# The residual of the first output projection: identity products in the sum's own bank, or transposes into a separate bank and an add on VectorE

## The chip, the core and the metric

The kernel runs on one core of a Trainium2 chip (trn2). The metric is the device time of one execution in microseconds (us). Before the change three runs took 3237.32, 3238.66 and 3239.86 us; their median is 3238.66 us.

## The reference

One step of a one-layer trunk over 640 frames: 512 of a prompt and 8 running streams of 16. With `h = rmsnorm(x)`, three mixers (GLA, gated delta net, RWKV-7) read columns of one projection `h @ w_in`, and then

```python
mix = jnp.matmul(jnp.concatenate([o_gla, o_gdn, o_rw], axis=-1), prm['w_out'][l])
x = x + mix
h = rmsnorm(x, prm['norm2_g'][l])
x = x + jnp.matmul(jax.nn.silu(jnp.matmul(h, w_ffn_gate)) * jnp.matmul(h, w_ffn_up), w_ffn_down)
y = rmsnorm(x, prm['final_norm_g'])
```

`x` is 640 x 2048 in float32, `w_out` 2048 x 2048. The change is in the line `x = x + mix`: how the old `x` gets into that sum.

## The kernel before

The kernel keeps activations transposed: 16 blocks of 128 columns, each a tile of 128 partitions x 640 frames. A float32 operand is split into a high part and the rest (`hi`, `lo`), and each product is three matmuls of 128x320: `hi` x high, `hi` x low, `lo` x high (lines 1388, 1389, 1390 in `dense`). They are called **dense products** below.

The stages follow each other: `norm1`, the mixers, the output projection in two halves (`outproj1` over 8 of the 16 blocks of the mixers' output, `outproj2` over the other 8), then the feed-forward part. The mixers' instructions all carry line 322, whatever they do; their order was worked out by a planner inside the program (class `Plan`). Everything behind them is put in order by the framework that builds the kernel: it takes an instruction when its inputs and its buffers are free, by priority, so `outproj1` starts while the last unit of the mixers (a gated delta head pair) still runs, and its dense products lie between that unit's small ones. Each engine then runs its list strictly in that fixed order, and waits where an instruction's inputs are late.

In PSUM the pool `pd` holds three tiles of 128x512 in float32, and the mixers' pool `mps` five (two `ma`, two `mm`, one `po`). `mps` is closed in `build` before `outproj1` is called; later pools get its places.

`outproj1` (line 1577) goes over 16 blocks m of output columns. For each it loads the 128 columns of `x` into a tile `xf` (frames on partitions, lines 1588 and 1590), loads two pieces of `w_out` and splits them (lines 1368, 1371 on ScalarE, 1372 on VectorE; three raw buffers and three `hi`/`lo` pairs in rotation), runs 48 dense products into two `pd` tiles (one for each half of the frames), and adds the residual: six products with the identity, `xf` as the left operand, which turn `xf` around and accumulate it into the same two `pd` tiles (line 1597; four of 128 columns, two of 64). Then ScalarE copies both halves over `xf` (line 1603). `mixparts` (lines 1570 to 1572) loads and splits the mixers' output. `outproj2` adds its own products to those tiles later with VectorE (line 1659).

Of the kernel before, what the change touches and what calls it, by code (L numbers as in the profile page):

```python
# [13 lines left out]
F32 = mybir.dt.float32  # L14
# [3 lines left out]
AF = mybir.ActivationFunctionType  # L18
ALU = mybir.AluOpType
AX = mybir.AxisListType  # L20
PSUM = bass.MemoryType.PSUM

T = 640
TP = 512
NT = 5
# [1313 lines left out]
class Trunk:  # L1339
# [70 lines left out]
    def build(self):  # L1410
        tc, nc, a, o = self.tc, self.nc, self.a, self.o
        ctx = ExitStack()
        with ctx:
            kp = ctx.enter_context(tc.tile_pool(name="kp", bufs=1))
            dp = ctx.enter_context(tc.tile_pool(name="dram", bufs=1, space=bass.MemoryType.DRAM))
            self.pd = ctx.enter_context(tc.tile_pool(name="pd", bufs=3, space=PSUM))
            ident = kp.tile([128, 128], F32, name="ident0")
            nc.sync.dma_start(out=ident, in_=self.cf_ap[:, CF_OFF["ident"][0]:CF_OFF["ident"][0] + 128])
            self.ident = ident
            mixd = dp.tile([16, 128, T], F32, name="mixd")  # L1420
            yd = dp.tile([16, 128, T], F32, name="yd")
            actd = dp.tile([22 * 7, 128, 320], F32, name="actd")
            mctx = ExitStack()
            bp = ctx.enter_context(tc.tile_pool(name="bp", bufs=1, side="right"))
            wctx = ExitStack()
            self.wp = wctx.enter_context(tc.tile_pool(name="wp", bufs=1, side="right"))
            self.free, self.where = [(bp, f"b{i}") for i in range(32)], {}
            h = [(self.take(), self.take()) for k in range(16)]
            self.cols = [kp.tile([128, sum(n for _, n in g)], F32, name=f"cols{i}") for i, g in enumerate(GROUPS)]
            self.norm1(h)  # L1430
            mc = mctx.enter_context(tc.tile_pool(name="mc", bufs=1))
            ms = mctx.enter_context(tc.tile_pool(name="ms", bufs=1))
            mps = mctx.enter_context(tc.tile_pool(name="mps", bufs=1, space=PSUM))
            self.mixers(h, mixd, (mc, ms, mps))
            self.give(*(t for x in h for t in x))
            mctx.close()
            bq = ctx.enter_context(tc.tile_pool(name="bq", bufs=1))
            places = [(bq, f"b{i}") for i in range(32, 57)]
            x2, xs = self.outproj1(mixd, KORDER, places)
            self.pe = ctx.enter_context(tc.tile_pool(name="pe", bufs=3, space=PSUM))  # L1440
            self.px = ctx.enter_context(tc.tile_pool(name="px", bufs=1, space=PSUM))
            self.fs = ctx.enter_context(tc.tile_pool(name="fs", bufs=1))
            with tc.tile_pool(name="fa", bufs=1) as self.fa:
                self.acts = Acts(self, actd)
                self.outproj2(KORDER[8:], xs, x2, self.col("norm2_g"), yd)
                self.gateup()
            wctx.close()
            self.down(yd)
# [125 lines left out]
            xs.append((hi, lo))  # L1574
        return xs

    def outproj1(self, mixd, ks, places):

        nc, a = self.nc, self.a
        ks, later = ks[:8], ks[8:]  # L1580
        xs = self.mixparts(mixd, ks)
        x2 = []
        for m in range(16):
            x = self.take()
            xf = x.bitcast(F32)
            with self.tc.high_priority(offset=WPRIO):
                c = slice(m * 128, (m + 1) * 128)
                nc.sync.dma_start(out=xf[:, 0:TP].rearrange("p (i c) -> p i c", i=4),
                                  in_=a["x_prompt"][0, :, c].rearrange("(i p) c -> p i c", p=128))
                nc.sync.dma_start(out=xf[:, TP:T], in_=a["x_sample"].rearrange("b t d -> (b t) d")[:, c])  # L1590

            def residual(ps):
                for i in range(NT):
                    for hf in range(2):
                        t0, t1 = max(128 * i, 320 * hf), min(128 * i + 128, 320 * hf + 320)
                        if t0 < t1:
                            nc.tensor.matmul(ps[hf][:, t0 - 320 * hf:t1 - 320 * hf], lhsT=xf[:, i * 128:(i + 1) * 128],
                                             rhs=self.ident[:, t0 - 128 * i:t1 - 128 * i], start=False,
                                             stop=t1 in (320, T))

            z = self.dense(self.wcols(a["w_out"][0], m * 128, ks), len(ks) // 4, self.halves(xs), extra=residual)
            for hf in range(2):
                nc.scalar.activation(xf[:, hf * 320:(hf + 1) * 320], z[hf], AF.Copy)
            x2.append(x)
            if m == 6:
                self.free += places
                xs2 = []
            if 6 <= m < 14:
                xs2 += self.mixparts(mixd, later[m - 6:m - 5])
        self.give(*(t for x in xs for t in x))  # L1610
        return x2, xs2
# [531 lines left out]
KORDER = [10, 11, 12, 13, 14, 15, 0, 1, 2, 3, 4, 5, 6, 7, 8, 9]  # L2143
# [31 lines left out]
```

## Time and profile before

| | |
|---|---|
| median of three runs | 3238.66 us |
| the profiled execution | 3239.36 us, span 3237.5 us |
| TensorE busy | 3162.8 us, 98% |
| TensorE weight loads | 3045.5 us, 94% |
| VectorE, ScalarE, GpSimd busy | 71%, 41%, 10% |
| granted TensorE clock, mean | 0.994 |
| HBM | 108 GB/s over the span |

A share of busy time is a mean over stages. A granted clock of 1.00 is the upper of TensorE's two levels (2.4 GHz), 0.50 the lower (1.2 GHz). Start times in a timeline are microseconds from the span's start; the time in brackets is idle time of that engine just before the row, with what ended it. A float32 product that isn't of the split kind is shown as two records, a transpose as one. The distance between the starts of two rows is what a product takes of the engine; the duration of a row includes the way through the array, and rows overlap.

### The profile page before, as it was taken

What the parts mean: (1) busy time and instruction counts of PE and PEld (TensorE: products, weight loads), DVE (VectorE), ACT (ScalarE), POOL (GpSimd) and SP (SyncE); (2) the same over time, 40 slices, a digit from 0 to 9 for tenths busy, and PEclk for the clock granted to TensorE, in tenths of its full rate; (3) what the DMA queues carried; (4) which work ended last, traced back from release to release, by engine and by line L of the source; (5) the groups of instructions that cost most, each with busy time, mean ns of one, the idle gap of its engine ahead of it and who ended that gap; (6) DMA issues with size and microseconds to landing.
All of it is one profiled execution on the core that took longest, in us unless ns stands there. A gap on an engine that the chain in (4) does not pass through costs nothing.

```text
span 3237.5 us, 61481 instructions
## 1 busy us (share of the span) xinstructions
PE 3162.8 (98%) x23589; PEld 3045.5 (94%) x23589; DVE 2307.0 (71%) x5672; ACT 1322.1 (41%) x2797; POOL 326.5 (10%) x521
## 2 busy tenths in 40 slices
PE   7999999999999999999999999999999999999997
PEld 6988888899999999999999999999999989999997
DVE  4677776664666677336888777777777788878786
ACT  4433333332333334335544344444443453434344
POOL 1111110000110000002000000000000032323221
PEclk9999999999999999999999999999999999999998
DMA  4222222222223235436433333333333376767675
GB/s 130 59 57 55 56 49 46 60 59 70 72 75 78 75 78 145 149 115 186 125 106 111 117 96 120 105 109 114 103 116 107 108 225 136 185 126 197 136 171 150
DMA packets 407528, 354.24 MB, mean 109 GB/s; under 512 B 26080, under 2 KB 390098, under 8 KB 406594
## 3 DMA queue, kind: packets, MB, share of 16 engines
q1 hardware_dynamic: 374098, 284.36, 30.3%
q0 software_dynamic: 32848, 65.96, 9.2%
q8 instruction: 184, 3.01, 0.4%
q14 instruction: 110, 0.90, 0.1%
q10 hardware_dynamic: 288, 0.01, 0.0%
HBM read 282.13 MB, written 68.11 MB: 108 GB/s over the span
## 4 chain that ended last, share of the span: by engine, by line
PE 84%; DVE 6%; issue 4%; DMA 3%; ACT 1%; POOL 1%; SPq 0%; DVEq 0%; POOLq 0%; ACTq 0%
PE d_r L322 22%; PE pw L1799 10%; PE pw L1800 10%; PE pw L1801 10%; PE mm_r L322 8%; PE dn L1962 4%; PE dn L1964 4%; PE dn L1963 4%; PE pd L1390 2%; PE pd L1388 2%; PE pd L1389 2%; PE ma_r L322 2%; PE po_r L322 1%; DMA dr<-in_w_ffn_down 1%; POOL yd L2066 1%
## 5 line engine op out<-in xcount | busy, mean ns | idle before, releaser
L322 PE MATMUL d_r<-b,hi_r 128*128 128x320 f32 (+1 forms) x3648 | 797.5, 317 | 0.7 <-ACT b L1529 0.7
L322 PEld LDWEIGHTS d_r<-b,hi_r 128*128 128x128 f32 (+1 forms) x3648 | 593.6, 188 | 22.4 <-issue 13.7
L322 PE MATMUL d_r<-b,lo_r 128*128 128x320 f32 (+1 forms) x1824 | 506.7, 317 | 0.0
L1799 PE MATMUL pw<-b,hi 128*128 128x320 f32 x1416 | 437.3, 309 | 0.0
L1800 PE MATMUL pw<-b,hi 128*128 128x320 f32 x1416 | 436.5, 308 | 0.2 <-DVE b L1635 0.2
L1801 PE MATMUL pw<-b,lo 128*128 128x320 f32 x1416 | 436.6, 308 | 0.0
L1963 PE MATMUL dn<-b,dh 128*128 128x320 f32 x1222 | 379.8, 311 | 7.3 <-DVE b L2104 7.3
L1964 PE MATMUL dn<-b,dl 128*128 128x320 f32 x1222 | 379.1, 310 | 7.2 <-DVE dl L1945 7.2
L1962 PE MATMUL dn<-b,dh 128*128 128x320 f32 x1222 | 378.7, 311 | 0.9 <-ACT dh L1944 0.9
L322 PEld LDWEIGHTS d_r<-b,lo_r 128*128 128x128 f32 (+1 forms) x1824 | 324.3, 188 | 7.5 <-issue 3.9
L1800 PE MATMUL pw<-b,hx 128*128 128x320 f32 x936 | 289.4, 309 | 0.0
L1799 PE MATMUL pw<-b,hx 128*128 128x320 f32 x936 | 289.2, 309 | 0.1
L1801 PE MATMUL pw<-b,lx 128*128 128x320 f32 x936 | 289.1, 309 | 0.0
L1800 PEld LDWEIGHTS pw<-b,hi 128*128 128x128 f32 x1416 | 265.5, 188 | 0.8 <-DVE b L1635 0.8
L1799 PEld LDWEIGHTS pw<-b,hi 128*128 128x128 f32 x1416 | 265.7, 188 | 0.2
L1801 PEld LDWEIGHTS pw<-b,lo 128*128 128x128 f32 x1416 | 265.7, 188 | 0.0
L322 DVE TENSOR_TENSOR lo_r<-raw_r,hi_r 128x512 fp32r<-128x512 f32 (+1 forms) x228 | 155.6, 683 | 145.3 <-ACT hi_r L322 104.8
L322 ACT ACTIVATE hi_r<-raw_r 128x512 fp32r<-128x512 f32 (+1 forms) x228 | 142.2, 624 | 256.4 <-PE d_r L322 236.3
L1963 PEld LDWEIGHTS dn<-b,dh 128*128 128x128 f32 x1222 | 230.3, 188 | 9.7 <-DVE b L2104 9.7
L1964 PEld LDWEIGHTS dn<-b,dl 128*128 128x128 f32 x1222 | 230.5, 189 | 8.4 <-DVE dl L1945 8.4
L1962 PEld LDWEIGHTS dn<-b,dh 128*128 128x128 f32 x1222 | 230.5, 189 | 1.4 <-ACT dh L1944 1.4
L1388 PE MATMUL pd<-b,hi 128*128 128x320 f32 x640 | 200.9, 314 | 3.4 <-ACT b L1571 1.9
(482 smaller groups left out, 6301.1 us busy)
## 6 DMA issues: line engine op xcount, KB each, us to landing
raw_r<-in_w_in SPq DMA_DIRECT2D x224, 256.0 KB
rw<-in_w_ffn_gate SPq DMA_DIRECT2D x84, 512.0 KB
rw<-in_w_ffn_up SPq DMA_DIRECT2D x84, 512.0 KB
b<-actd POOLq DMA_DIRECT2D x77, 320.0 KB, 7.0
dr<-in_w_ffn_down SPq DMA_DIRECT2D x32, 768.0 KB
actd<-s SPq DMA_DIRECT2D x132, 160.0 KB
raw<-in_w_out SPq DMA_DIRECT2D x80, 256.0 KB
yd<-t POOLq DMA_DIRECT2D x124, 160.0 KB, 4.8
```

What stands on the lines that cost most here:

```text
L322: self.made.append(op[2](*op[3], **op[4]))
L1388: nc.tensor.matmul(out, lhsT=hi[:, kk, :], rhs=xh, start=k == 0, stop=False)
L1389: nc.tensor.matmul(out, lhsT=hi[:, kk, :], rhs=xl, start=False, stop=False)
L1390: nc.tensor.matmul(out, lhsT=lo[:, kk, :], rhs=xh, start=False, stop=k == nk - 1 and not extra)
L1799: nc.tensor.matmul(ps, lhsT=hi[:, kk, :], rhs=bh, start=k == 0, stop=False)
L1800: nc.tensor.matmul(ps, lhsT=hi[:, kk, :], rhs=bl, start=False, stop=False)
L1801: nc.tensor.matmul(ps, lhsT=lo[:, kk, :], rhs=bh, start=False, stop=k == 7)
L1962: nc.tensor.matmul(ps, lhsT=hi[:, k], rhs=bh, start=k == 0, stop=False)
L1963: nc.tensor.matmul(ps, lhsT=hi[:, k], rhs=bl, start=False, stop=False)
L1964: nc.tensor.matmul(ps, lhsT=lo[:, k], rhs=bh, start=False, stop=k == c - 1)
L2066: nc.gpsimd.dma_start(out=yd[2 * p + i // 2][:, ones(i)], in_=z, accum_op=ALU.add)
```

## The change

The dense products of a block end the sum by themselves. The residual no longer goes through products with the identity: five transposes turn `xf` around into a PSUM tile of its own (`pt`, 640 columns of a 1024 column tile in a new pool `xt` with one buffer). ScalarE copies each half of `pt` over `xf`, and VectorE adds the `pd` tile to it.

```diff
-            x2, xs = self.outproj1(mixd, KORDER, places)
+            with tc.tile_pool(name="xt", bufs=1, space=PSUM, reuse_waits="tile") as xt:
+                x2, xs = self.outproj1(mixd, KORDER, places, xt)
...
-    def outproj1(self, mixd, ks, places):
+    def outproj1(self, mixd, ks, places, xt):
...
-            def residual(ps):
-                for i in range(NT):
-                    for hf in range(2):
-                        t0, t1 = max(128 * i, 320 * hf), min(128 * i + 128, 320 * hf + 320)
-                        if t0 < t1:
-                            nc.tensor.matmul(ps[hf][:, t0 - 320 * hf:t1 - 320 * hf], lhsT=xf[:, i * 128:(i + 1) * 128],
-                                             rhs=self.ident[:, t0 - 128 * i:t1 - 128 * i], start=False,
-                                             stop=t1 in (320, T))
-
-            z = self.dense(self.wcols(a["w_out"][0], m * 128, ks), len(ks) // 4, self.halves(xs), extra=residual)
+            z = self.dense(self.wcols(a["w_out"][0], m * 128, ks), len(ks) // 4, self.halves(xs))
+            pt = xt.tile([128, 1024], F32, name=self.name("xt"), tag="x")[:, 0:T]
+            for i in range(NT):
+                c = slice(i * 128, (i + 1) * 128)
+                nc.tensor.transpose(pt[:, c], xf[:, c], self.ident)
             for hf in range(2):
-                nc.scalar.activation(xf[:, hf * 320:(hf + 1) * 320], z[hf], AF.Copy)
+                c = slice(hf * 320, (hf + 1) * 320)
+                nc.scalar.activation(xf[:, c], pt[:, c], AF.Copy)
+                nc.vector.tensor_tensor(xf[:, c], xf[:, c], z[hf], ALU.add)
```

The lists of the engines move. In the changed file the lines behind `build` carry other numbers: 1597 is the transpose, 1600 ScalarE's copy, 1601 VectorE's add.

TensorE, where the last mixer unit's first correction products come (`mm_r` from `X_r` and `N_r`; `pd` are tiles of the dense products). Before:

```order
L1388 MATMUL pd_13436<-b_13251,hi_13440 128x320
L1389 MATMUL pd_13436<-b_13252,hi_13440 128x320
L322 MATMUL mm_r_400<-X_r_407,N_r_415 128x64 x4
L1390 MATMUL pd_13436<-b_13251,lo_13441 128x320
L1388 MATMUL pd_13437<-b_13233,hi_13440 128x320
L1389 MATMUL pd_13437<-b_13234,hi_13440 128x320
L1390 MATMUL pd_13437<-b_13233,lo_13441 128x320
L322 MATMUL mm_r_401<-Y_r_404,P_r_406 128x64 x4
L1388 MATMUL pd_13437<-b_13239,hi_13440 128x320
```

With the change:

```order
L1390 MATMUL pd_13365<-b_13272,lo_13403 128x320
L1388 MATMUL pd_13365<-b_13278,hi_13402 128x320
L1389 MATMUL pd_13365<-b_13279,hi_13402 128x320
L1390 MATMUL pd_13365<-b_13278,lo_13403 128x320
L322 MATMUL mm_r_400<-X_r_407,N_r_415 128x64 x4
L322 MATMUL mm_r_401<-Y_r_404,P_r_406 128x64 x4
L322 MATMUL mm_r_400<-X_r_407,N_r_415 64x32 x8
L322 MATMUL mm_r_401<-Y_r_404,P_r_406 32x32
L322 MATMUL mm_r_400<-P_r_406,Y_r_404 64x32 x8
```

Before, dense products of the blocks m = 2 and on stand between the mixers' products. With the change 72 dense products (48 of block 0 and the first half of the frames of block 1, tile `pd_13365`) stand ahead of this place, and none between the mixers' products from here on.

TensorE, at the mixers' last two products (`mm_r` from `SX_r` and `VS_r`). Before:

```order
L1388 MATMUL pd_13588<-b_13245,hi_13592 128x320
L322 MATMUL mm_r_400<-SX_r_410,VS_r_398 128x512
L1389 MATMUL pd_13588<-b_13246,hi_13592 128x320
L1390 MATMUL pd_13588<-b_13245,lo_13593 128x320
L1388 MATMUL pd_13588<-b_13251,hi_13592 128x320
L1389 MATMUL pd_13588<-b_13252,hi_13592 128x320
L1390 MATMUL pd_13588<-b_13251,lo_13593 128x320
L1388 MATMUL pd_13589<-b_13233,hi_13592 128x320
L322 MATMUL mm_r_401<-SX_r_410,VS_r_398 128x512
L1389 MATMUL pd_13589<-b_13234,hi_13592 128x320
```

With the change:

```order
L322 MATMUL mm_r_401<-ident_63,on_r_416 128x128
L322 MATMUL mm_r_400<-ident_63,on_r_416 128x128 x4
L322 MATMUL mm_r_400<-SX_r_410,VS_r_398 128x512
L322 MATMUL mm_r_401<-SX_r_410,VS_r_398 128x512
L1597 MATMUL xt_13352<-ident_63,b_13284 128x128 x5
L1597 MATMUL xt_13430<-ident_63,b_13362 128x128 x3
L1388 MATMUL pd_13366<-b_13236,hi_13369 128x320
L1389 MATMUL pd_13366<-b_13237,hi_13369 128x320
L1390 MATMUL pd_13366<-b_13236,lo_13370 128x320
```

Before, block 4 has begun by the mixers' last product (`pd_13588`, `pd_13589`), and four blocks have their residual. With the change the first transposes of all, those of block 0, stand behind the mixers' last product, and the second half of block 1 (`pd_13366`) behind them.

VectorE, later in `outproj1`, where the loop runs evenly (blocks 12 and 13), with the change:

```order
L1601 TENSOR_TENSOR b_14256<-b_14256,pd_14259 128x320
L1601 TENSOR_TENSOR b_14256<-b_14256,pd_14260 128x320
L1372 TENSOR_TENSOR lo_14465<-raw_14459,hi_14464 128x512
L1372 TENSOR_TENSOR lo_14510<-raw_14507,hi_14509 128x512
L1601 TENSOR_TENSOR b_14340<-b_14340,pd_14343 128x320
L1601 TENSOR_TENSOR b_14340<-b_14340,pd_14344 128x320
```

Before, VectorE's list has only the `lo` splits here; now two adds follow two splits in each block. From the first rows of `outproj2` to the end of the kernel, TensorE, VectorE and ScalarE have the same lists before and after, and GpSimd's is the same throughout; SyncE's differs in the places of some loads within `outproj1`.

## Rows read from the trace of the kernel before

**Rows 1.** Busy time of each engine, from the profile's page.

```profile
PE 3162.8 (98%) x23589; PEld 3045.5 (94%) x23589; DVE 2307.0 (71%) x5672; ACT 1322.1 (41%) x2797; POOL 326.5 (10%) x521
```

**Rows 2.** Busy time by engine, clock, DMA share in two windows of `outproj1`.

```profile
1288.50:1323.15 34.65, 34.46 (x281) 30.84 (x281) 15.16 (x38) 11.45 (x35) 1.12 (x2) 1.00 0.16 50
...
1324.40:1422.00 97.60, 97.60 (x702) 97.60 (x701) 21.20 (x30) 29.34 (x53) 1.04 (x3) 1.00 0.47 139
```

**Rows 3.** TensorE's timeline around a block's residual: start, duration, engine, line, operation.

```profile
1330.09 0.31 PE L1389 MATMUL pd<-b,hi 128*128 128x320 f32 x1
...
1336.83 0.31 PE L1390 MATMUL pd<-b,lo 128*128 128x320 f32 x1
1336.98 1.50 PE L1597 MATMUL pd<-ident,b 128*128 128x128 f32 x12
1338.23 0.39 PE L1388 MATMUL pd<-b,hi 128*128 128x320 f32 x1
1338.46 0.31 PE L1389 MATMUL pd<-b,hi 128*128 128x320 f32 x1
```

**Rows 4.** TensorE's timeline in norm1: five transposes between dense products.

```profile
30.14 0.31 PE L322 MATMUL d_r<-b,hi_r 128*128 128x320 f32 x1
30.29 0.71 PE L1522 MATMUL xpa<-ident,x 128*128 128x128 f32 x5
30.75 0.39 PE L322 MATMUL d_r<-b,hi_r 128*128 128x320 f32 x1
30.98 0.71 PE L1522 MATMUL xpa<-ident,x 128*128 128x128 f32 x5
```

**Rows 5.** Line 322 alone (the mixers): PE, PEld, DVE, ACT, POOL busy.

```profile
1281.30:1288.50 7.20, 0.00 (x1) 0.01 (x1) 5.05 (x43) 0.00 (x0) 0.53 (x1) 1.00 0.50 147
1288.50:1323.15 34.65, 19.29 (x158) 14.90 (x158) 11.92 (x33) 7.38 (x27) 1.12 (x2) 1.00 0.16 50
```

**Rows 6.** Lines 1388, 1389, 1390 alone: PE busy and count, PEld, until 1322.51.

```profile
1255.00:1322.51 67.51, 22.63 (x69) 12.91 (x69) 1.00 0.49 141
...
1255.00:1322.51 67.51, 22.05 (x68) 12.88 (x68) 1.00 0.49 141
...
1255.00:1322.51 67.51, 21.51 (x68) 12.83 (x68) 1.00 0.49 141
```

**Rows 7.** VectorE's and TensorE's timelines: the mixers' last chain, first and last steps.

```profile
1287.14 0.68 DVE L1372 TENSOR_TENSOR lo<-raw,hi 128x512 fp32r<-128x512 f32 x1
...
1288.50 1.10 PE L322 MATMUL mm_r<-X_r,N_r 128*128 128x64 f32 x8 [0.43 <-DVE X_r L322]
...
1319.14 0.60 PE L322 MATMUL mm_r<-ident,on_r 128*128 128x128 f32 x4
...
1320.60 1.12 PE L322 MATMUL mm_r<-SX_r,VS_r 128*128 128x512 f32 x2
...
1322.51 1.13 PE L322 MATMUL mm_r<-SX_r,VS_r 128*128 128x512 f32 x2
```

**Rows 8.** TensorE's timeline after an idle stretch, and a window of it.

```profile
1589.27 0.41 PE L1390 MATMUL pd<-b,lo 128*128 128x320 f32 x1 [2.47 <-DVE lo L1372]
...
1589.89 0.47 PE L1390 MATMUL pd<-b,lo 128*128 128x320 f32 x1
...
1593.26 0.30 PE L1388 MATMUL pd<-b,hi 128*128 128x320 f32 x1
...
1590.00:1592.00 2.00, 2.00 (x9) 2.00 (x8) 2.00 (x5) 0.00 (x0) 0.00 (x0) 0.50 0.51 146
```

**Rows 9.** ScalarE's copies and VectorE's split in a steady block; outproj2's add.

```profile
1338.01 0.94 ACT L1603 ACTIVATE b<-pd 128x320 f32<-128x320 f32 x2 [0.35 <-PE pd L1597]
...
1337.69 0.69 DVE L1372 TENSOR_TENSOR lo<-raw,hi 128x512 fp32r<-128x512 f32 x1 [2.83 <-ACT hi L1371]
...
L1603 ACT ACTIVATE b<-pd x32: 429/438/439, 1279.1 to 1422.3; 128x320 f32<-128x320 f32 x32
...
L1659 DVE TENSOR_TENSOR b<-b,pd x32: 469/487/490, 1425.8 to 1538.3; 128x320 f32<-128x320 f32 x32
```

## The prediction, made blind

> **What bounds the kernel now.** I read the page's busy times first: TensorE is busy for 98% of the span [rows 1], so what the change takes from TensorE or leaves it without work counts in full, unless something else ends a stage. Then the windows of this stage. From 1324.40 to 1422.00 us, most of `outproj1`, TensorE is busy for all 97.60 us, VectorE for 21.20, and the DMA engines for 0.47 of the time [rows 2]: TensorE alone is the bound there. Just before, while the last mixer unit finishes, TensorE is busy for 34.46 of 34.65 us as well [rows 2], but the reader should then look at the mixers' line alone: of these 34.65 us it fills 19.29, and from 1281.30 to 1288.50 it has no time on TensorE at all, while VectorE solves for `X_r` [rows 5]. What fills the rest is dense products and residuals of `outproj1`. They are a filler under a chain of small steps over TensorE, ScalarE and VectorE. Last I read the timelines, for what one piece takes and for what the chain waits on.
>
> **What the change removes.** Where the loop runs evenly a block's residual begins at 1336.98, where the next dense product would have stood (the one before began at 1336.83). The two dense products after it begin at 1338.23 and 1338.46 [rows 3]. So the way from 1336.98 to 1338.46 took 1.48 us with one dense product in it; dense products follow each other every 0.147 us (46 steps within a block, from 1330.09 to 1336.83 [rows 3]). The residual costs TensorE 1.33 us a block.
>
> **What it adds on TensorE.** Five float32 transposes of 128x128 stand between dense products in `norm1`: they begin at 30.29, the next dense product at 30.75 and what follows it at 30.98 [rows 4]. That is 0.69 us with one dense product in it, so 0.54 us a block. Each block thus saves 0.79 us, and 16 blocks 12.6 us, if nothing else moved. The Trainium skill, "TensorE: Matmul & The Clock Gate", section "Terms", says that transpose mode is four times as fast for float32. Both forms stream 640 columns, so by that rule a block's transposes would take 0.33 us and 16 blocks would save 16.0 us; the rows have a fixed part at each change of kind, and I stay with 0.54.
>
> **What it adds elsewhere.** ScalarE still copies two halves a block, 0.438 us each [rows 9]; only the source is another. VectorE gets 32 adds, of 0.487 us as in `outproj2` [rows 9], 15.6 us on an engine busy for 21.20 of 97.60 [rows 2]. They cost nothing as long as the `pd` tile is free in time. Block m+1 begins in the third tile, twelve dense products long, and then needs the tile of block m's first half. Counted from the end of block m's products, that need comes at 0.54 + 12 x 0.147 = 2.30 us. The tile is free after the transposes (0.46), the hand-over to ScalarE (0.35, the idle time in rows 9), the copy (0.44) and the add (0.49), 1.74 us, and about 1.9 with two short hand-overs. VectorE's list puts two splits ahead of the adds. The last of them began 0.71 us after the residual (1337.69 against 1336.98) and took 0.69 [rows 3, 9], so it ends at about 1.4 and the add at 1.9. The cover is 0.4 us; a further split in front would cost 0.3 us in that block.
>
> **What it moves, the large term.** The list of TensorE shows that all transposes stand behind the mixers' last product. Block 0 can't be finished without them, so its two `pd` tiles stay full, the first half of block 1 takes the third, and TensorE has run out of filler after 48 + 24 = 72 dense products. Before, by the mixers' last product at 1322.51 [rows 7], the three lines of the dense products had 69 + 68 + 68 = 205 records [rows 6], and four blocks had their residual. So 133 dense products, 133 x 0.147 = 19.5 us, lose their cover and come after the chain instead. Of the residuals, the four that lay under the chain gave nothing when removed; the other twelve give 12 x 1.33 = 16.0 us. All 16 sets of transposes come after it: 16 x 0.54 = 8.6 us. From this alone the end comes 19.5 - 16.0 + 8.6 = **12.1 us later**.
>
> **Three corrections.** First, the chain itself. Without dense products on TensorE and splits on VectorE in its way it gets shorter: the first `SX_r` products came at 1320.60, though what precedes them had run from 1319.14 for 0.60, so 0.86 us of filler lay between. A split of 0.68 ended just ahead of the `X_r` that TensorE waited for at 1288.50 [rows 7]. With a split earlier in the same stretch and smaller delays of the same kind I take 3 us. It can hardly be much more: the mixers' own times on TensorE, VectorE and ScalarE from 1288.50 to 1323.15 add up to 19.29 + 11.92 + 7.38 = 38.6 us in a window of 34.65 [rows 5], so little of it is waiting for others. Bounds: 0 and 8. Second, the restart. After the first transposes TensorE waits for a copy and an add (0.35 + 0.44 + 0.49 and two hand-overs, about 1.4 us) and has 0.3 us of block 1's transposes meanwhile: 1.1 us, once.
>
> Third, the clock. In this trace 2.47 us without work before 1589.27 were followed by 13 dense products in the 3.37 us from 1589.89 to 1593.26, 0.26 us each instead of 0.147, with a granted clock of 0.50, the 1.2 GHz level [rows 8]. That cost 3.37 - 1.91 = 1.5 us. With the change TensorE has nothing to do for the 7.2 us up to 1288.50, so the mixers' products that follow start at the lower level. Then they fill a little more than half of the time, and no row shows which level holds in such a stretch. Lower bound: one such drop, 1.5 us. Upper bound: all 19.29 us of the mixers on TensorE at half speed, 19.3 us more, the drop after it included. The row nearest to it is that of the single drop, which ended after 3.4 us of full work; here there is no full work until the end. Some of the products also lie beside the chain. I take a third, **6.5 us**. The Trainium skill, "TensorE: Matmul & The Clock Gate", section "HAM oscillation — how this bites in real kernels", describes that short bursts between waits start cold each time. By that rule the whole chain would run at the lower level, which is a rival below; rows 8 show the drop, and no run here shows such bursts.
>
> **The sum.** 12.1 - 3.0 + 1.1 + 6.5 = 16.7 us on the profiled execution's 3239.36: 3256.1. That execution is 0.7 above the median of the runs, 3238.66, so I predict 3255. What follows `outproj1` is in the same order as before, so I carry no later gain or loss.
>
> **The rivals.**
> - **One drop of the clock only.** TensorE returns to the upper level within the chain, as it did at 1593.26 [rows 8], and the term is 1.5: 12.1 - 3.0 + 1.1 + 1.5 = 11.7, so 3250. For it: the mixers take more than half of the time at full speed. Against: 7.2 us of nothing first, and every step waits for another engine. 0.21.
> - **The lower clock all along the chain.** About three quarters of the 19.29 us lie on the chain and double, 14 us, and the restart pays a drop of 1.5: 12.1 - 3.0 + 1.1 + 15.5 = 25.7, so 3264. The Trainium skill's rule, named above, would come out here. For it: no stretch of full work between 1288.50 and the transposes. 0.17.
> - **The bare chain contracts.** If the chain was slow because it queued behind filler, it ends much earlier alone. At the upper clock 12.1 + 1.1 = 13.2 us of contraction brings the time to 3239, and 20 us to 3232, faster than before. It decides from 13 us on. Against: its own work fills the window [rows 5], and TensorE waited for the chain, not the other way, where it began [rows 7]. 0.11 for anything near or beyond no change.
> - **The add holds the banks.** If VectorE is late by another split in each of 14 blocks, 14 x 0.3 = 4 us come on top, 3260. It is inside the range.
> - That the change doesn't do what it says I leave out: the lists have 16 sets of five transposes and 32 adds.
>
> **How the numbers follow.** The forecast, a clock that is low for part of the chain (3252 to 3261), has 0.51. The range 3245 to 3266 takes in the single drop, the forecast, and most of the low clock; it leaves out the contracting chain and the far end of the low clock, 0.17 together. This kernel's measurement tells about 0.2% (6.5 us) from no change: faster means under 3232, slower over 3245. Only a chain shorter by 20 us is faster, 0.03; the rest of that rival, and a single drop with a chain shorter than I take it, is the same, 0.09; all else is slower, 0.88.
>
> **What the profile after would show.** TensorE idle from about 1281 to 1288, with the wait put down to VectorE's `X_r`, and then line 322 alone until about 1320 to 1335, with gaps. The granted clock below 1.00 in that stretch is the third correction; its mean tells which of the three cases holds. The first transposes follow the `SX_r` products; from there a block takes 48 x 0.147 + 0.54 = 7.6 us in place of 8.4, with no waits of dense products on VectorE's adds. `outproj1` ends some 17 us later than before, and the rest keeps its length. I am wrong if dense products run between the mixers' products after 1290, if the clock stays at 1.00 through the idle stretch, if the blocks take over 7.7 us, or if the later stages change their length by over 2 us.

## The result, and the profile after

The changed kernel takes 3269.24 us (median of four runs, 3266.97 to 3270.61), the kernel before 3239.05 (four runs on the same chip, 3237.32 to 3239.86). The ratio is 1.0094, with a 95% interval from 1.0082 to 1.0106: slower by some 30 us. The forecast was 3255, its range ended at 3266. The sign is right; the size lies above the range.

The profiled execution took 3270.17 us with a span of 3268.2. The page's busy times answer to [rows 1]:

```profile
PE 3171.2 (97%) x23477; PEld 3048.8 (93%) x23477; DVE 2321.7 (71%) x5704; ACT 1320.3 (40%) x2797; POOL 326.2 (10%) x521
```

TensorE has 112 records fewer (12 per block for the residual before, 5 now) and is busy for 8.4 us *more*. Fewer records and more busy time point to work that ran slower; the rows below show where. TensorE's timeline from the hole to the restart answers to [rows 7] (start, duration, engine, line, operation; in brackets the idle time and what ended it):

```profile
1279.81 0.31 PE L1390 MATMUL pd<-b,lo 128*128 128x320 f32 x1
1288.00 1.97 PE L322 MATMUL mm_r<-X_r,N_r 128*128 128x64 f32 x8 [7.88 <-DVE X_r L322]
...
1327.37 1.44 PE L322 MATMUL mm_r<-ident,on_r 128*128 128x128 f32 x5 [3.88 <-ACT on_r L322]
1329.66 2.08 PE L322 MATMUL mm_r<-SX_r,VS_r 128*128 128x512 f32 x2 [0.84 <-DVE G_r L322]
1332.52 2.08 PE L322 MATMUL mm_r<-SX_r,VS_r 128*128 128x512 f32 x2 [0.79 <-DVE SX_r L322]
1334.39 1.27 PE L1597 MATMUL xt<-ident,b 128*128 128x128 f32 x5
1336.52 0.90 PE L1597 MATMUL xt<-ident,b 128*128 128x128 f32 x3 [0.85 <-ACT b L1600]
1337.07 0.62 PE L1388 MATMUL pd<-b,hi 128*128 128x320 f32 x1
```

TensorE runs out of dense products at 1280, waits 7.9 us for `X_r`, and has the mixers' chain alone until 1332.52, 10.0 us later than before (the chain begins 0.5 us sooner and is 10.5 us longer). Each of these mixers' rows takes almost twice as long as its counterpart in [rows 7]: 1.97 for 1.10, 2.08 for 1.13. The windows of TensorE give the reason (window, its length, busy time and records, granted clock, DMA share, GB/s):

```profile
1280.00:1284.00 4.00, 0.12 (x1) 0.83 0.97 278
1284.00:1288.00 4.00, 0.00 (x1) 0.50 0.01 2
1288.00:1292.00 4.00, 3.47 (x15) 0.50 0.00 0
...
1316.00:1320.00 4.00, 4.00 (x19) 0.50 0.00 0
...
1340.00:1344.00 4.00, 4.00 (x28) 0.91 0.50 138
1344.00:1348.00 4.00, 4.00 (x30) 1.00 0.82 240
```

From 1284 to 1340 all 14 windows of 4 us have a granted clock of 0.50, the 1.2 GHz level. Line 322 alone in the chain (busy time of PE, PEld, DVE, ACT, POOL), which answers to [rows 5]:

```profile
1288.00:1334.60 46.60, 34.70 (x158) 25.80 (x158) 11.99 (x33) 7.46 (x27) 1.11 (x2) 0.50 0.02 9
```

The same 158 records of TensorE, 34.70 us where they took 19.29; VectorE and ScalarE need what they needed before. Behind the restart the loop runs as forecast. TensorE's timeline around a block's transposes, first where it is disturbed and then in the even part:

```profile
1364.72 0.71 PE L1597 MATMUL xt<-ident,b 128*128 128x128 f32 x5
...
1368.45 0.42 PE L1388 MATMUL pd<-b,hi 128*128 128x320 f32 x1 [0.96 <-DVE b L1601]
...
1373.54 0.71 PE L1597 MATMUL xt<-ident,b 128*128 128x128 f32 x5
...
1388.71 0.71 PE L1597 MATMUL xt<-ident,b 128*128 128x128 f32 x5
1389.17 0.39 PE L1388 MATMUL pd<-b,hi 128*128 128x320 f32 x1
1389.41 0.30 PE L1389 MATMUL pd<-b,hi 128*128 128x320 f32 x1
...
1396.29 0.71 PE L1597 MATMUL xt<-ident,b 128*128 128x128 f32 x5
```

From 1388.71 to 1389.41 is 0.70 us with one dense product in it: 0.55 for the transposes. A block takes 7.58 us (1388.71 to 1396.29). Before it took 8.37, from the residual at 1336.98 [rows 3] to the next one in TensorE's timeline:

```profile
1345.35 1.50 PE L1597 MATMUL pd<-ident,b 128*128 128x128 f32 x12
```

So the even part saves the forecast 0.79 us a block. One block takes 8.82, from 1364.72 to 1373.54, because a dense product waits for VectorE's add (line 1601).

To see in which stage the time lies, three starts are read from TensorE's timeline of each kernel: the first `X_r,N_r` product, the last `SX_r,VS_r` product, and the first product of the feed-forward part's main loop (tile `pw`). Their differences, and the rest of the span, for all kernels of this study (the labels are explained below; the columns are what the starts give, in us):

| kernel | chain: first `X_r,N_r` to last `SX_r,VS_r` | output projection: from there to the first `pw` product | from there to the end of the span |
|---|---|---|---|
| before | 1288.50 to 1322.51: 34.0 | to 1604.7: 282.2 | to 3237.5: 1632.8 |
| after | 1288.00 to 1332.52: 44.5 | to 1632.8: 300.3 | to 3268.2: 1635.4 |
| filler (e1) | 1282.52 to 1316.32: 33.8 | to 1614.5: 298.2 | to 3251.6: 1637.1 |
| identity, own bank (e2) | 1284.07 to 1328.57: 44.5 | to 1636.5: 307.9 | to 3273.9: 1637.4 |
| transposes from block 4 (e3) | 1284.70 to 1318.70: 34.0 | to 1594.1: 275.4 | to 3231.9: 1637.8 |
| transposes from block 3 (e4) | 1284.99 to 1319.04: 34.1 | to 1592.6: 273.6 | to 3227.7: 1635.1 |
| transposes from block 1 (e5) | 1285.89 to 1328.26: 42.4 | to 1623.2: 294.9 | to 3258.9: 1635.7 |
| transposes from block 2 (e6) | 1287.51 to 1322.86: 35.4 | to 1606.8: 283.9 | to 3240.5: 1633.7 |
| as e4, block 7 by identity (e7) | 1287.79 to 1321.83: 34.0 | to 1594.3: 272.5 | to 3230.0: 1635.7 |

Between before and after, 10.5 us are in the chain, 18.1 in the output projection behind it, 2.6 in what follows. In that last part TensorE's list is the same in before and after, and its length varies over the table from 1632.8 to 1637.8 with no relation to the edits; the profile of before has the shortest. The part ahead of the chain has its own spread too: the mixers' last dense product of line 322 (`d_r`) comes between 1258.5 and 1262.9.

### The profile page after: what moved, and what is told of

It reads as the page before. It is cut to its first block, busy times and chain, and to the rows that moved or that the text cites. A ratio compares the mean times of both kernels' runs of the same rounds, so it can differ in the third digit from the quotient of the medians.

```text
span 3268.2 us, 61325 instructions
## 1 busy us (share of the span) xinstructions
PE 3171.2 (97%) x23477; PEld 3048.8 (93%) x23477; DVE 2321.7 (71%) x5704; ACT 1320.3 (40%) x2797; POOL 326.2 (10%) x521
## 4 chain that ended last, share of the span: by engine, by line
PE 84%; DVE 6%; issue 4%; DMA 3%; ACT 2%; POOL 1%; SPq 0%; DVEq 0%; POOLq 0%; ACTq 0%
PE d_r L322 22%; PE pw L1797 10%; PE pw L1798 10%; PE pw L1799 10%; PE mm_r L322 9%; PE dn L1960 4%; PE dn L1962 4%; PE dn L1961 4%; PE pd L1390 2%; PE pd L1388 2%; PE pd L1389 2%; PE ma_r L322 2%; PE po_r L322 1%; DMA b<-actd 1%; DMA dr<-in_w_ffn_down 1%
```

## The experiments

The theory after reading the two profiles: the wait for the bank leaves a hole in TensorE's list; in the hole the chain is alone, the clock falls and nearly doubles the time of the chain's products; each block behind it does save 0.79 us. The rivals: the separate bank, the copy and the add slow the chain or the loop in themselves; and, within the theory, that it is the 7.9 us of standing still, not the bare chain (the chain without dense products between its steps), that costs the clock. One step is not tested here by itself: that the first transposes stand behind the mixers' last product because `xt` finds its place only where `mps` was. This is read from the code and the lists. In every kernel here with `xt` they stand behind it, and none gave `xt` a place sooner.

**e1, a filler in the hole.** Against the changed kernel (cut; the last line passes `again` to `dense`, which runs it ahead of the `lo` product that ends block 1's first half):

```diff
...
+            again = None
+            if m == 1:
+                def again(ps, hi):
+                    for r in range(130):
+                        nc.tensor.matmul(ps[0][:, 0:320], lhsT=hi[:, r % 4, :], rhs=xs[r % 8][0][:, 0:320], start=False, stop=False)
...
+            z = self.dense(self.wcols(a["w_out"][0], m * 128, ks), len(ks) // 4, self.halves(xs), again=again)
```

> The changed kernel with 130 extra products of 128 x 320, of the dense kind, written behind block 1's first products and put by the scheduler on TensorE's queue where the change left a hole: 42 ahead of the first X_r,N_r product and the rest between the mixers' last products, until on_r. They do nothing of use: they add to the first half of block 1 a term that the reference does not have, so that half is changed. Theory (the chain of the mixers takes 10 us longer because the clock falls to 1.2 GHz when TensorE has nothing but that chain to do): the granted clock stays at 1.00 from 1280 to 1340, the first wait on X_r vanishes, the last SX_r,VS_r product is back at 1320 to 1325 (1332.5 in the changed kernel, 1322.5 before), the restart is at full speed, and the time is 3239.1 + 12.1 (the lost cover less the saved products) + 1 to 3 = 3252 to 3254; with the 2 to 3 us that the later stages were longer, up to 3257. Rival (the chain is longer for another reason: the add, the copy or the transposes in their own bank keep VectorE and ScalarE from the mixers' work): the clock is at 1.00 but the last SX_r,VS_r product stays past 1330, and the time at 3267 to 3271.

Measured: 3252.78 us (3251.62 to 3265.49), ratio to before 1.0051 (1.0033 to 1.0070). TensorE's windows:

```profile
1284.00:1288.00 4.00, 4.00 (x41) 1.00 0.00 0
...
1308.00:1312.00 4.00, 2.62 (x17) 1.00 0.00 0
1312.00:1316.00 4.00, 2.11 (x7) 1.00 0.07 27
1316.00:1320.00 4.00, 2.82 (x16) 1.00 0.16 61
```

TensorE's timeline at the chain's first and last products:

```profile
1282.52 1.10 PE L322 MATMUL mm_r<-X_r,N_r 128*128 128x64 f32 x8 [0.87 <-DVE X_r L322]
...
1316.32 1.12 PE L322 MATMUL mm_r<-SX_r,VS_r 128*128 128x512 f32 x2 [0.78 <-DVE SX_r L322]
```

130 products whose only effect on the result is a term that the reference does not have, 19 us of TensorE at 0.147 each, make the changed kernel 14 to 16 us faster (by the two ratios, 0.0043 of 3238, or by the medians). The clock is 1.00 in the whole chain, and the chain takes 33.8 us, as before. So the 10.5 us come from TensorE having nothing else to do there, and neither from the bank, the copy nor the add. What is left against before is 14.7 us by the medians. By the profiles the output projection is 16.0 us longer (298.2 against 282.2): the predicted 12.1, a wait of 0.9 at the restart, a late add of 1.9, and some 1.5 for a drop of the clock behind it (shown at the end).

**e2, the price of the transposes.** Against the changed kernel:

```diff
-                nc.tensor.transpose(pt[:, c], xf[:, c], self.ident)
+                nc.tensor.matmul(pt[:, c], lhsT=xf[:, c], rhs=self.ident, start=True, stop=True)
```

> The changed kernel with the five transposes of each block replaced by five fp32 products with the identity into the same bank of its own; copy and add as in the changed kernel, the instructions in the same order. Theory (a block's transposes take 0.54 us of TensorE, its products with the identity 1.1 to 1.33 us, and TensorE has no time to spare in the first output projection): 16 x 0.57 to 0.79 us more, with two blocks of them at half the clock: 3269.2 + 9 to 14 = 3278 to 3283. Rival (what the change saves is not the transposes' price but the place in the accumulation, and TensorE waits for ScalarE and VectorE in each block anyhow): within 3 us of the changed kernel, 3266 to 3272.

Measured: 3274.10 us (3271.24 to 3276.53), ratio to before 1.0108 (1.0094 to 1.0122). By the time alone it falls between the two. TensorE's timeline:

```profile
1387.46 1.27 PE L1597 MATMUL xt<-ident,b 128*128 128x128 f32 x10
...
1395.61 1.27 PE L1597 MATMUL xt<-ident,b 128*128 128x128 f32 x10
```

A block takes 8.15 us in place of 7.58, so 0.57 more, the lower price of the theory; 16 of them are 9.1 us. The output projection grew by only 7.6 (307.9 against 300.3), since here the dense products ran at full speed from the first one at the restart, where the changed kernel had 13 at half speed (1.6 us, below). In the profiled execution the chain also started 3.9 us sooner than in that of the changed kernel. The price holds at its lower end. The total, 4.9 us above the changed kernel, lies below the 9 to 14 that the theory gave: the restart accounts for 1.6 of that, and the earlier start is one execution's, so for the median the rest is not explained.

**e3 and e4, transposes only where the cover is not touched.** Against the kernel before, with `residual` as it was there (cut; the pool `xt` and the loop of transposes are those of the change; `late = m >= 3` in e4):

```diff
...
+            late = m >= 4
+            z = self.dense(self.wcols(a["w_out"][0], m * 128, ks), len(ks) // 4, self.halves(xs),
+                           extra=None if late else residual)
+            if late:
+                pt = xt.tile([128, 1024], F32, name=self.name("xt"), tag="x")[:, 0:T]
...
+                nc.scalar.activation(xf[:, c], pt[:, c] if late else z[hf], AF.Copy)
+                if late:
+                    nc.vector.tensor_tensor(xf[:, c], xf[:, c], z[hf], ALU.add)
```

> Blocks 0 to 3 keep the products with the identity, accumulated, as before; blocks 4 to 15 take the transposes into the bank of their own and the add. The bank is then first asked for after the mixers' products have ended, so their chain keeps the dense cover and its place. Theory (the loss is all in the hole that the wait for the bank leaves, and each of the 12 blocks behind it saves 0.79 us): no wait on X_r at 1280 to 1288, the clock at 1.00, the last SX_r,VS_r product at 1322 to 1323, and the time 3239.1 - 12 x 0.79 = 3229.6; with one add that is late by 1 to 2 us, or with 2 to 3 us of longer later stages, up to 3234. Rival (the add and its bank cost more than the transposes save, and the hole was only part): 3239 or more.

> As the kernel with blocks 0 to 3 on the identity, but from block 3 on with transposes: block 3's transposes then stand on TensorE right behind the mixers' last products, and its finished sums wait for the add. Theory: 13 x 0.79 saved, 3228.8, and the cover of the chain whole, since the dense products of blocks 0 to 3 go ahead as before; up to 3234 with the same late add and later stages. Rival (the held sums of block 3 take a buffer that the next block's products need, so a piece of the cover is lost): a wait of 1 to 8 us on TensorE before 1322, a granted clock under 1.00 if it is long, and 3231 to 3245.

Measured: e3 3231.86 us (3227.52 to 3234.98, 11 runs), ratio 0.9977 (0.9968 to 0.9986); e4 3231.13 us (3227.99 to 3231.66, 8 runs), ratio 0.9977 (0.9966 to 0.9987). Both are faster than the kernel before, by about 7 us, and by some 38 us than the changed one. TensorE's waits in e4 from 1255 to 1460 (us in total, times, longest):

```profile
PE pd L1388 <- ACT b L1572: 1.9, 1, 1.9
PE mm_r L322 <- ACT on_r L322: 1.5, 2, 1.1
PE pd L1388 <- DVE b L1614: 1.5, 1, 1.5
PE mm_r L322 <- DVE X_r L322: 0.9, 1, 0.9
PE xt L1609 <- ACT b L1612: 0.9, 1, 0.9
```

No wait for `X_r` beyond 0.9 us, the clock at 1.00 from 1272 to 1364 in every window of 4 us, the chain at 34.0 and 34.1. In e4 eight more dense products stand ahead of the chain's end than before (213 against 205), and 13 sets of transposes replace the twelve residuals behind it: -8 x 0.147 - 16.0 + 13 x 0.54 = -10.2, and with the late add (line 1614 there) of 1.5 and the wait of 0.9 at the second block's transposes (line 1609) it makes -7.8. Measured: 273.6 - 282.2 = -8.6. In e3, which has no such wait, -16.0 + 12 x 0.54 + 1.7 = -7.8 was due and -6.8 came. The prices thus come out to within 1 us. The rivals, an add that costs more than the transposes save and held sums that break the cover, fall.

**e5, the bare chain without the standing still.** As e3, with one number changed:

```diff
-            late = m >= 4
+            late = m >= 1
```

> Block 0 alone keeps the products with the identity; blocks 1 to 15 take the transposes into their own bank. On TensorE some 20 dense products still stand beside the first X_r,N_r products, so that the engine has work while the first X_r is being made and the 7.9 us of standing still are gone; behind them the chain of the mixers is as bare as in the changed kernel (5 of 98 dense products in it). What it separates: does the clock fall because TensorE stands still for 8 us, or because the chain is bare? Theory A (the bare chain alone is enough): the clock falls to 0.50 some microseconds into the chain and stays there to its end, the chain is 8 to 10 us longer, and the time is 3238.1 + 12.5 (85 dense products that lost their cover, at 0.147) - 11.9 (15 x 0.79) + 8 to 13 = 3247 to 3252. Theory B (it is the standing still that starts it): the clock stays at 1.00, the chain ends no later than before or up to 3 us sooner, and the time is 3235 to 3240.

Measured: 3258.79 us (3255.51 to 3260.73), ratio 1.0059 (1.0047 to 1.0071). TensorE's timeline at the chain's start:

```profile
1285.89 1.10 PE L322 MATMUL mm_r<-X_r,N_r 128*128 128x64 f32 x8 [0.28 <-DVE X_r L322]
...
1288.44 0.39 PE L1390 MATMUL pd<-b,lo 128*128 128x320 f32 x1
1289.89 0.66 PE L322 MATMUL mm_r<-X_r,N_r 64*64 64x32 f32 x16 [1.06 <-DVE X_r L322]
1290.98 0.25 PE L322 MATMUL mm_r<-Y_r,P_r 64*32 64x32 f32 x2 [0.43 <-ACT P_r L322]
1291.28 1.07 PE L322 MATMUL mm_r<-P_r,Y_r 64*64 64x32 f32 x16
```

TensorE's windows in the same kernel:

```profile
1284.00:1288.00 4.00, 3.72 (x27) 1.00 0.21 61
1288.00:1292.00 4.00, 2.46 (x39) 0.91 0.02 5
1292.00:1296.00 4.00, 2.83 (x34) 0.50 0.00 0
```

The 7.9 us are gone, the first products of the chain run at full speed (1.10), and still the clock falls soon after the last dense product, at 1288.44, is through: sixteen small products take 0.66 us at 1289.89, and sixteen of the same size 1.07 at 1291.28. It stays at 0.50 to the chain's end, which comes after 42.4 us instead of 34.0. Theory A holds: here the bare chain is enough, without a long wait ahead of it. The time lies above its 3247 to 3252, because I had counted 0.79 saved for each of the 15 blocks. Three of these blocks had their residual under the chain before, for nothing; by the prediction's own way of counting, 12.5 - 16.0 + 15 x 0.54 = +4.6, not +0.6. With 8.4 in the chain, 2.3 for the late add, some 3.8 for the restart and some 1.4 for a drop of the clock behind the late add it is +20.5; the stages show 8.4 + 12.7 = +21.1.

**e6, half of the chain bare.** The same line with `late = m >= 2`.

> Blocks 0 and 1 keep the products with the identity; blocks 2 to 15 take the transposes. 61 of the 98 dense products stay between the first X_r,N_r product and the last SX_r,VS_r one, all but the last 12 steps of the chain, which are bare. Lost cover 37 x 0.147 = 5.4, saved 14 x 0.79 = 11.1. Theory A (a bare piece of the chain lowers the clock): the clock is below 1.00 from about 1308 to the end of the chain and the restart, 1 to 4 us more, one late add 1.7: 3238.1 - 5.7 + 2.7 to 5.7 = 3235 to 3238. Theory B (only standing still for long does): clock 1.00 but for one step, 3232 to 3235. In both cases slower than the kernels that keep four or three blocks on the identity (3231.1 to 3231.9), which keep the cover whole.

Measured: 3242.55 us (3238.42 to 3249.43, 12 runs), ratio 1.0015 (1.0006 to 1.0024). TensorE's timeline at the end of the chain:

```profile
1313.04 0.80 PE L322 MATMUL mm_r<-dl_r,G_r 128*128 128x128 f32 x2 [0.23 <-ACT dl_r L322]
1317.71 1.44 PE L322 MATMUL mm_r<-ident,on_r 128*128 128x128 f32 x5 [3.88 <-ACT on_r L322]
```

TensorE's windows there:

```profile
1308.00:1312.00 4.00, 3.13 (x24) 1.00 0.02 7
1312.00:1316.00 4.00, 1.51 (x6) 0.63 0.03 9
1316.00:1320.00 4.00, 1.44 (x5) 0.50 0.00 0
```

The last dense product in the chain is at 1307.99; from about 1313 the clock is at 0.50, later than the 1308 that was expected, and the chain takes 1.4 us more than before. Theory A again, but how soon the clock falls is open: in e1 the last 6.7 us of the chain, from 1310.6, had no dense product either and kept 1.00. The time lies above the 3235 to 3238 by the same mistake in the sum: 5.4 - 16.0 + 14 x 0.54 = -3.0, not -5.7; with 2.0 for the late add, 0.9 for a wait at the second block's transposes, 1.5 for the last `SX_r,VS_r` pair and five transposes at the lower clock (0.95 + 0.54) and 1.4 in the chain it is +2.8. The stages show 35.4 + 283.9 against 34.0 + 282.2, so +3.1.

**e7, the late add.** Against e4:

```diff
-            late = m >= 3
+            late = m >= 3 and m != 7
```

> The kernel with transposes from block 3 on, but block 7 too keeps the products with the identity. In each kernel with the change TensorE waits once, for 1.0 to 2.3 us, on a late add, and it is block 7's: ScalarE's copy of that block stands behind pieces of the mixed values whose transfers it waits for, and the add behind the copy holds the bank that the dense products want next. Theory (the wait comes from the copy and the add being two steps behind those pieces): with the identity, block 7 frees its bank with one copy, the wait is gone or under 0.5 us, and the time is 3231.1 - 1.5 + 0.79 = 3230.4, not to be told from the kernel it comes from (3231.1). Rival (ScalarE is late whatever the block does): the wait stays at 1 to 2 us, now on ScalarE's copy of block 7, and the time is 3231.1 + 0.79 = 3231.9.

Measured: 3230.65 us (3226.61 to 3234.25, 11 runs), ratio 0.9974 (0.9965 to 0.9983). TensorE's waits from 1255 to 1460 hold no add any more, and none on block 7's copy:

```profile
PE mm_r L322 <- ACT on_r L322: 1.7, 2, 1.3
PE xt L1609 <- ACT b L1612: 0.9, 1, 0.9
```

ScalarE's timeline in the same kernel shows that it was late all the same:

```profile
1351.57 1.54 ACT L1572 ACTIVATE b<-b 128x640 fp32r<-128x640 f32 x2 [1.76 <-DMA b<-mixd]
1353.01 0.62 ACT L1371 ACTIVATE hi<-raw 128x512 fp32r<-128x512 f32 x1
1353.53 0.74 ACT L1612 ACTIVATE b<-pd 128x320 f32<-128x320 f32 x2
```

It waits 1.76 us for the mixers' output from memory, then works off two pieces and a weight split before block 7's copy. With one step behind that the bank is free in time here; in e4, with two (copy, then add), it was not. Two things differ, though: the products with the identity also hold TensorE 0.79 us longer than transposes, so the bank is wanted later. How much each gives is not shown. The time cannot be told from e4's, as both theories had it; the wait decides.

The expectation has one thing wrong. Counted by the dense products ahead of it, the late add is block 7's only in e3 and e4. In the changed kernel and in e1 it is block 4's, in e2 block 3's, in e5 block 5's, in e6 block 6's: whichever block is done when ScalarE waits for the mixers' output. The step from e4 to e7 is not touched by this. By its median e7 is the fastest of the kernels here, but e3, e4 and e7 are not apart from each other.

## Why the prediction was right in sign and too low

The steps in the order of the prediction, in us; "measured" is the profile after against the profile before.

| step | predicted | measured |
|---|---|---|
| 133 dense products lose their cover | +19.5 | +19.5: 72 dense products ahead of the last `SX_r,VS_r` product, 205 before [rows 6] |
| twelve residuals, sixteen sets of transposes | -16.0 + 8.6 | -16.0 + 8.6: 0.79 saved a block in the even part |
| chain: contraction and clock | -3.0 + 5.0 | +10.0 (10.5 longer, begun 0.5 sooner) |
| restart, and the drop of the clock at it | +1.1 + 1.5 | +4.2 |
| adds of VectorE | 0 | +1.2, in one block |
| rest of the output projection | 0 | +0.6 |
| later stages | 0 | +2.6 |
| sum | +16.7 | +30.7 |

**Right: the hole and what it moves.** Nothing of TensorE's list came otherwise than read: 72 dense products, the wait put down to VectorE's `X_r`, line 322 alone to 1332.52, the first transposes behind it, 7.58 us a block where 7.6 was forecast. The 0.79 us saved a block is what the even part shows (8.37 against 7.58). In e2, 0.57 of it is there for five products each way; e3 and e4 come out with it to within 1 us.

**Wrong: the third correction, the clock.** This is the step that failed. The prediction took "a third, 6.5 us" between 1.5 and 19.3, because the nearest row was the single drop [rows 8], which ended with full work. The rival "The lower clock all along the chain" is what happened: 0.50 in all 14 windows from 1284 to 1340, 15.4 us more for the mixers on TensorE (34.70 against 19.29), of which 10.5 reach the chain's length. The rival had 14 less 3.0 of contraction for that, so 11, and a time of 3264; it had a chance of 0.17. Even that is short of the measured time, because it still took off the contraction and had one drop at the restart. The row I leaned on was not like this case: after that drop TensorE had nothing but dense products to do, here it had nothing but a chain in which it often waits. The Trainium skill, "TensorE: Matmul & The Clock Gate", section "HAM oscillation — how this bites in real kernels", tells of bursts of products between waits for transfers, each of which starts at the lower clock. This trace agrees as to the clock (0.50 throughout); but its waits are for other engines, and in e5 none of those shown ahead of the fall was longer than 1.06 us, which is shorter than the waits of the page's example. The prediction carried that rule over to this chain and gave it too small a chance.

**Mis-sized: the restart.** The wait at the first copy was 0.85 us, near the 1.1 forecast. But the products around it also ran at the lower clock: 0.95 more for the last `SX_r,VS_r` pair, about 0.8 for the first eight transposes, and 1.6 for 13 dense products at 0.267 us each, until about 1340.6. That makes 4.2.

**Missed: one late add.** In 15 blocks no dense product waits for an add. In block 4 ScalarE is late with the copy, since it waits for the mixers' output from memory ahead of it. ScalarE's timeline in the changed kernel:

```profile
1364.98 1.55 ACT L1572 ACTIVATE b<-b 128x640 fp32r<-128x640 f32 x2 [1.47 <-DMA b<-mixd]
1366.44 0.62 ACT L1371 ACTIVATE hi<-raw 128x512 fp32r<-128x512 f32 x1
1366.96 0.74 ACT L1600 ACTIVATE b<-xt 128x320 f32<-128x320 f32 x2
```

The rival "The add holds the banks" did not see this: it looked at VectorE's splits, not at what ScalarE waits for. In the changed kernel it costs 1.2 us (8.82 against 7.58, a wait of 0.96 in it); in e1 to e6 the wait is 1.2 to 2.3.

**Not an effect that is shown: the later stages.** I had said that a change of over 2 us there would prove me wrong. It is 2.6, but kernels that differ only in the output projection have it anywhere between 0.9 and 5.0 above the profile of before, so one pair of profiles can't tell it from chance.

**Left open: the contraction.** No kernel here has the bare chain at the full clock; with the filler at the full clock it took 33.8 us, with VectorE's splits out of its way, so the 3.0 that I took off are neither shown nor refuted.

## What to carry to other kernels

A filler under a chain of small dependent steps does two things: its own work is free there, and it keeps TensorE's clock up for the chain. So before a new buffer is asked for, look at when it becomes free, and at what stands behind the instruction that waits for it; here a bank that came free more than 40 us too late for the first blocks (their residual stood at 1278 before, the first transposes now at 1334.39) turned a saving of 0.79 us a block into a loss of 30 us. Do such a change only from the iteration on at which the buffer is there (e4). Price a stretch that loses its filler at the lower clock as the bad case: it came out so in the changed kernel, in e2 and in e5, for the last part of it in e6, and not at the end of e1.

## What was not expected of the hardware

- The clock did not come back although TensorE was busy: in the changed kernel the window from 1316 to 1320 has 4.00 us of busy time out of 4.00, all of the mixers' small products, and 0.50; the windows around it have 2.8 to 3.5. With a filler of dense products the same chain had windows of 2.11 and 2.82 us (e1, 1312 to 1320) and kept 1.00, behind one of 2.62 us and full ones up to 1308.
- Waits of nearly 2 us in the middle of dense products can go either way. In e1 a late add of 1.87 us was followed by some 12 dense products at half speed; in e3 one of 1.75 us and in e6 one of 1.96 us left the clock at 1.00. TensorE's timeline in e1:

```profile
1349.81 0.58 PE L1388 MATMUL pd<-b,hi 128*128 128x320 f32 x1 [1.87 <-DVE b L1608]
...
1352.59 0.47 PE L1389 MATMUL pd<-b,hi 128*128 128x320 f32 x1
```

- Executions of these kernels reach the mixers' last `d_r` product 4.4 us apart (1258.5 to 1262.9), ahead of all that the edits move on TensorE and more than several of the effects above. So lengths of stages tell more here than points in time.
